# Row scales through DRAM, and squares summed on token-major rows, in a hybrid encoder layer

## The chip, the cores and the metric

The kernel runs on one core of one Trainium2 chip. The metric is the device time of one execution in microseconds (us). The three runs of the kernel before took 768.85, 768.90 and 769.19 us; the median is 768.9.

## The reference, cut to what matters

One layer of an encoder over x (512 tokens, width 1024, float32). What the change touches are two of its norms:

```python
def rmsnorm(x, g):
    xf = x.astype(jnp.float32)
    y = xf * lax.rsqrt(jnp.mean(xf * xf, axis=-1, keepdims=True) + EPS)
    return (y * g.astype(jnp.float32)).astype(x.dtype)

hn = rmsnorm(h, norm_mix_g[l])
proj = hn @ w_in[l]
...
h = h + memory_cross_attention(rmsnorm(h, norm_x_g[l]), mem_n, w_xq[l], w_xkv[l], w_xo[l])
u = rmsnorm(h, norm_ff_g[l]) @ w1[l]
h = h + jnp.square(jax.nn.relu(u)) @ w2[l]
return rmsnorm(h, final_norm_g)
```

Between them stand eight heads of attention with a forget bias, a gated recurrence (HGRN2) over chunks, and attention to 256 memory tokens. The hidden width of the MLP is 4096.

## The kernel before, in words

Activations stand feature-major: 128 features on the partitions, 512 tokens along the free dimension, eight such chunks for the width of 1024. Every matrix product is made of three matmuls per chunk, with each operand split into a high and a low part (`gemm_fm`, lines 236 to 238; 24 matmuls for one product of 128 output features by 512 tokens). Weights come by DMA from SP's queue into two raw buffers, are split by ACT (line 171, names wh) and DVE (line 175, names wl), and the load of the next panel waits for the split of the last but one. PE's order is the order of the code; the other engines are ordered by a scheduler, except in a few blocks written out by hand.

The row scale of a norm is not applied to the activations before the product. The gain is folded into the feature-major activations; the row scale, one number per token, multiplies the product afterwards. Since tokens lie along the free dimension there, the scale must stand in all partitions: a tile `rbc` of 128 x 512, each row the same.

**First norm.** Squares of x are summed on token-major x by ACT and DVE (`x_sq`), which gives `ms0`, 128 x 4, tokens on the partitions. POOL makes the power (`rstd_of`, lines 357 and 360). PE then spreads the 4 columns `r0` to all partitions by four transposes of a broadcast column (line 516, into a PSUM bank of pool `sc`), and DVE copies the bank to `rbc` (line 518). `gate` (line 540) multiplies the first four products `gf` by `rbc`; ACT's sigmoid follows, then `forget`, then the products `gq`. The four `gf` and `gq0` lie in the three banks of the PSUM pool `mm`. Beside this, `x_park` writes the transposed x to DRAM (xTd) from POOL's queue, in four transfers, and POOL loads the bias `fb`.

**MLP's norm.** After cross attention, `residual` adds each chunk of the product with W_xo (names xw) to the residual `hT`, makes the high and low parts `x2_hi` and `x2_lo`, and POOL squares the chunk and adds it to `ssq2` (lines 1073, 1076 and 1077). When three, five and seven chunks are done, `to_tok` transposes two chunks to the token-major accumulator `acc`, whose four tiles (one per 128 tokens) collect the MLP's output; the last two chunks follow after the first product of the MLP. `mean_sq` (line 1087) sums `ssq2` over the partitions on PE by small matmuls, POOL makes the power, and PE and DVE spread the scale as before (lines 1507 and 1508) into the same tile `rbc`. `square` (lines 1305 and 1308) takes max(u, 0) times `rbc` on DVE and squares on ACT, and this frees the product's bank.

**The MLP.** The hidden width is done in eight groups of four products u (group g, half j, column i), with three banks of pool `mm`. For the second matrix, tiles of W2 (names wq) are loaded by SP (`load_raws`), and POOL issues DMAs that add further tiles on top of them (`add_weights`, line 1245), since the product with W2 is made of seven products of sums. `first_adds` issues the first two of a group; `down_raws` is the load followed by them.

Of the kernel before, what the change touches and what calls it, by code (L numbers as in the profile page):

```python
# [42 lines left out]
def emit(  # L43
# [310 lines left out]
    def rstd_of(ms, n, name, r=None):  # L354
# [5 lines left out]
        gp.tensor_tensor(r, e, mhalf[:, 0:n], op=ALU.pow)  # L360
        return r

    def norm_rows(t, name):
        ms = sm(2, name + "m")
        for i in range(2):
            junk = t2(f"{name}j{i}")
            ac.activation(junk, t[:, i * S : (i + 1) * S], AF.Square, scale=1.0 / 32.0, accum_out=ms[:, i : i + 1])
        ve.tensor_tensor(ms[:, 0:1], ms[:, 0:1], ms[:, 1:2], ALU.add)
        r = rstd_of(ms[:, 0:1], 1, name + "r")
        ve.tensor_scalar(t, t, r, None, op0=ALU.mult)  # L370
# [67 lines left out]
    with tc.manual_schedule(engines={mybir.EngineType.Activation, mybir.EngineType.DVE}):  # L438
        ve.tensor_copy(g_mix, gmp)
        x_T(0)  # L440
        warm = mm("warm2")
        for _ in range(WARM2):
            te.matmul(warm, zero[:, 0:P], zero, start=True, stop=True)
        first[0]("v")
        x_hi(0)
        x_lo(0)
        first[0]("l")
        wt0 = stream[0]
        state["used"] = 1
        gfps = [mm(f"gf{i}") for i in range(2)]  # L450

        def first_rows(w, a, start):
            for i in range(2):
                te.matmul(gfps[i], chunk(w, 0, slice(i * P, (i + 1) * P)), a[:, 0, :], start=start, stop=False)

        first_rows(wt0[0], hn_hi, True)
        x_T(1)
        x_hi(1)
        x_lo(1)
        first_rows(wt0[0], hn_lo, False)  # L460
        first_rows(wt0[1], hn_hi, False)
        gfg = [gemm_fm(gfps[i], wt0, i * P, hn_hi, hn_lo, order=range(1, KC), begun=True) for i in range(2)]
        second = []

        def l_soft():

            gps = sc("gps", (33,))
            te.transpose(gps, rows, ident[0:33, 0:33])
            ve.tensor_copy(gv, gps)
            ve.tensor_tensor(lmx, gv[:, 25:29], gv[:, 29:33], ALU.max)  # L470
            ve.tensor_tensor(le, gv[:, 25:33].rearrange("p (r k) -> p r k", r=2), lmx.unsqueeze(1).to_broadcast([P, 2, 4]), ALU.subtract)
            ac.activation(le, le, AF.Exp)
            ve.tensor_tensor(lden, le[:, 0, :], le[:, 1, :], ALU.add)
            ve.reciprocal(lden, lden)
            ve.tensor_tensor(lb, le[:, 0, :], lden, ALU.mult)
            ve.tensor_scalar(oml, lb, -1.0, 1.0, op0=ALU.mult, op1=ALU.add)

        jobs = (
            (first[1],),
            (lambda: x_park(0), lambda: x_park(1), first[2]),  # L480
            (first[3], lambda: second.extend(load_next())),
            (lambda: x_sq(0), lambda: x_park(3)),
            (lambda: x_park(2), lambda: second[0]("h"), lambda: x_sq(2)),
            (lambda: x_sq(1), lambda: second[0]("l"), lambda: x_sq(3)),
            (lambda: second[1]("hl"), l_soft),
            (),
        )
        for c in range(KC):
            for g in gfg if c else ():
                next(g)  # L490
            if c + 2 < KC:
                x_T(c + 2)
                x_hi(c + 2)
                x_lo(c + 2)
            for job in jobs[c]:
                job()
        for g in gfg:
            assert next(g, None) is None
        x_park(7)

        wt1 = stream[1]
        state["used"] = 2
        third = load_next()
        gfps.append(mm("gf2"))
        gf2 = gemm_fm(gfps[2], wt1, 0, hn_hi, hn_lo)
        for _ in range(GF):
            next(gf2)
        r0 = cp.tile([P, NT], F32, name="r0")
        rstd_of(ms0, NT, "r0", r0)

        fb = cp.tile([P, FH], F32, name="fb")
        gp.tensor_copy(fb[:, 0:NT], r0)
        gp.dma_start(fb, fox_f_bias[0].partition_broadcast(P))
        pb = sc("rbc")
        for tb in range(NT):
            te.matmul(pb[:, tb * P : (tb + 1) * P], r0[:, tb : tb + 1].to_broadcast([P, P]), ident, start=True, stop=True)
        rbc = cp.tile([P, S], F32, name="rbc")
        ve.tensor_copy(rbc, pb)
        run_now(gf2)
        gfps.append(mm("gf3"))  # L520
        gf3 = gemm_fm(gfps[3], wt1, P, hn_hi, hn_lo)


        Fg, Mv, Sa, Ag = [], [], [], []
        for hp in range(2):
            Fg.append(s4([2, S], f"F{hp}"))
            Mv.append(s4([2, S], f"mov{hp}"))
            Sa.append(s4([2, S], f"sta{hp}"))

        def kt_(h):  # L530
            return (Sa, Mv)[h % 2][h // 2][:, h % 2, :]

        def qt_(h):
            return (Mv, Sa)[h % 2][h // 2][:, h % 2, :]


        sg = [t2(f"sg{h}") for h in range(4)]

        def gate(h):
            ve.tensor_tensor(sg[h], gfps[h], rbc, ALU.mult)  # L540
            ac.activation(sg[h], sg[h], AF.Sigmoid)

        def forget(h):
            F_ = Fg[h // 2][:, h % 2, :]
            ac.activation(F_, sg[h], AF.Identity, scale=oml[:, h : h + 1], bias=lb[:, h : h + 1])
            ac.activation(kt_(h), F_, AF.Identity, scale=-1.0, bias=1.0)

        x_park(4)
        x_park(6)
        gate(0)  # L550
        gate(1)
        x_park(5)
        third[0]()
        third[1]()
        run_now(gf3)
        gate(2)
        for h in range(3):
            forget(h)
# [3 lines left out]
    for hp in range(2):  # L562
        wt = next_panel()
        for j in range(2):
            h = 2 * hp + j
            ps = mm(f"gq{h}")
            run_now(gemm_fm(ps, wt, j * P, hn_hi, hn_lo))
            ve.tensor_tensor(qt_(h), ps, rbc, ALU.mult)
            ac.activation(qt_(h), qt_(h), AF.Silu)
# [476 lines left out]
    def residual(src_hi, src_lo, g, dst_hi, dst_lo, name, ssq, order, nlast, after=None):  # L1046
# [16 lines left out]
        def rest():  # L1063
            for c in range(KC):
                if c not in gens:
                    open_(c)
                yield from gens[c]
                hc = hTc(c)
                ve.tensor_tensor(hc, hc, ps_[c], ALU.add)  # L1069
                ac.activation(dst_hi[:, c, :], hc, AF.Identity, scale=g[:, c : c + 1])  # L1070
                ve.scalar_tensor_tensor(dst_lo[:, c, :], hc, g[:, c : c + 1], f(dst_hi[:, c, :]), op0=ALU.mult, op1=ALU.subtract)
                if c == 0:
                    gp.tensor_tensor(ssq, hc, hc, op=ALU.mult)
                else:
                    sq = t2(f"{name}sq{c}")
                    gp.tensor_tensor(sq, hc, hc, op=ALU.mult)
                    gp.tensor_tensor(ssq, ssq, sq, op=ALU.add)
                if after is not None and c in (2, 4, 6):
                    after(c - 2)
                    after(c - 1)  # L1080
# [85 lines left out]
    def to_tok(c):  # L1166
# [3 lines left out]
        for tb in range(NT):  # L1170
            d, s_ = acc[tb][:, c * P : (c + 1) * P], ps[:, tb * P : (tb + 1) * P]
            if tb % 2 == 0:
                ac.activation(d, s_, AF.Copy)
            else:
                ve.tensor_copy(d, s_)

    fill.add(x_proj(1), "xq1")
    fill.run(2.0)
    for h in range(4):
        if 0 < h < 3:  # L1180
            fill.add(x_proj(h + 1), f"xq{h + 1}")
        elif h == 3:
            x2_hi, x2_lo = act_tile("x2_hi"), act_tile("x2_lo")
            ssq2 = t2("ssq2")
            early, rest = residual(o_hi, o_lo, g_ff, x2_hi, x2_lo, "xw", ssq2, range(KC), 2, to_tok)
            fill.add(early())
        x_scores(h, 0)
        fill.run(X1)
# [107 lines left out]

    def mlp_up(g, j, wt):
        for i in range(2):
            ps = mm(f"u{g}{j}{i}")
            run_now(gemm_fm(ps, wt, i * P, x2_hi, x2_lo))  # L1300
            yield g, j, i, ps

# [171 lines left out]
    def mlp_up_group(g):  # L1474
        for j in range(2):
            if g < 2:
                wt = next_panel()
                if (g, j) == (0, 0):
                    down_raws(0)
                elif (g, j) == (1, 1):  # L1480
                    for _ in range(2):
                        unit_q.popleft()[1]()
# [14 lines left out]
    rbc2 = rbc  # L1497
    ups = mlp_up_group(0)
    up0 = next(ups)
    ms2 = mean_sq(ssq2, "pm2")  # L1500
    r2 = rstd_of(ms2, NT, "r2")
    to_tok(KC - 2)
    to_tok(KC - 1)
    up1 = next(ups)
    pb = tr("rbc2")
    for tb in range(NT):
        te.matmul(pb[:, tb * P : (tb + 1) * P], r2[:, tb : tb + 1].to_broadcast([P, P]), ident, start=True, stop=True)
    ve.tensor_copy(rbc2, pb)
    square(*up0)
    square(*up1)  # L1510
    for up in ups:
        square(*up)
    hidden_sums(0)
    for name in PRODUCTS:
# [42 lines left out]
```

## Time and profile before

| | us |
|---|---|
| median of three runs | 768.9 |
| the profiled execution's own time | 769.28 |
| its span, first to last instruction | 767.5 |
| busy in it: PE / DVE / ACT / POOL | 759.0 / 523.7 / 368.7 / 190.5 |

The granted clock of TensorE was 0.998 of full speed. In the profile PE is TensorE, DVE VectorE, ACT ScalarE, POOL GpSimd and SP the engine that issues most loads. A row of the timeline has start, duration, engine, line, operation, output and inputs with their shapes, and how many instructions were merged; in brackets stands the idle time ahead of it and what ended it. Matmuls overlap, so the cost of one is the distance between starts. A row of stretches has, after the span, the busy time of PE, of its weight loads, of DVE, ACT and POOL (instructions in parentheses), then the granted clock, the mean busy share of the 16 DMA engines and GB/s. A row of DMA issues ends with the us to landing, the median where there are several.

### The profile page before, as it was taken

What the parts mean: (1) busy time and instruction counts of PE and PEld (TensorE: products, weight loads), DVE (VectorE), ACT (ScalarE), POOL (GpSimd) and SP (SyncE); (2) the same over time, 40 slices, a digit from 0 to 9 for tenths busy, and PEclk for the clock granted to TensorE, in tenths of its full rate; (3) what the DMA queues carried; (4) which work ended last, traced back from release to release, by engine and by line L of the source; (5) the groups of instructions that cost most, each with busy time, mean ns of one, the idle gap of its engine ahead of it and who ended that gap; (6) DMA issues with size and microseconds to landing.
All of it is one profiled execution on the core that took longest, in us unless ns stands there. A gap on an engine that the chain in (4) does not pass through costs nothing.

```text
span 767.5 us, 11244 instructions
## 1 busy us (share of the span) xinstructions
PE 759.0 (99%) x4229; PEld 646.0 (84%) x4229; DVE 523.7 (68%) x849; ACT 368.7 (48%) x620; POOL 190.5 (25%) x264
## 2 busy tenths in 40 slices
PE   9999999999999999999999999999999999999996
PEld 6889888998889988888888888888888888888885
DVE  5747765576787656555548556949596868777696
ACT  5655456665666433344444244435353535342553
POOL 7207432423432025310016510101001010101123
PEclk9999999999999999999999999999999999999999
DMA  8543332232543442231113596565748475757602
GB/s 247 192 136 108 90 84 56 80 114 57 185 149 134 163 139 83 85 100 64 56 56 108 204 262 139 146 158 175 180 149 200 139 174 161 192 137 218 138 1 109
DMA packets 79831, 103.03 MB, mean 134 GB/s; under 512 B 4593, under 2 KB 58394, under 8 KB 79778
## 3 DMA queue, kind: packets, MB, share of 16 engines
q1 hardware_dynamic: 70226, 76.61, 31.1%
q0 software_dynamic: 8960, 24.67, 15.3%
q10 hardware_dynamic: 592, 1.05, 0.4%
q8 instruction: 33, 0.54, 0.3%
q14 instruction: 20, 0.16, 0.1%
HBM read 89.71 MB, written 4.21 MB: 122 GB/s over the span
## 4 chain that ended last, share of the span: by engine, by line
PE 98%; DVE 1%; ACT 1%; POOL 0%; issue 0%; DVEq 0%; ACTq 0%
PE u L238 8%; PE u L236 8%; PE u L237 8%; PE U L1371 4%; PE U L1369 4%; PE U L1370 4%; PE xq L236 2%; PE xq L237 2%; PE xw L236 2%; PE xq L238 2%; PE xw L237 2%; PE xw L238 2%; PE wo L236 2%; PE Y L1371 2%; PE wo L238 2%; PE Y L1370 2%
## 5 line engine op out<-in xcount | busy, mean ns | idle before, releaser
L175 DVE TENSOR_TENSOR wld<-wq,whd 128x1024 fp32r<-128x1024 f32 x56 | 68.6, 1226 | 25.3 <-ACT whd L171 25.2
L236 PE MATMUL u<-x_hi,whu 128*128 128x512 f32 x192 | 74.7, 389 | 0.0
L237 PE MATMUL u<-x_lo,whu 128*128 128x512 f32 x192 | 74.7, 389 | 0.0
L238 PE MATMUL u<-x_hi,wlu 128*128 128x512 f32 x192 | 74.7, 389 | 0.0
L171 ACT ACTIVATE whd<-wq 128x1024 fp32r<-128x1024 f32 x56 | 58.4, 1054 | 30.2 <-PE u L237 18.5
L171 ACT ACTIVATE whu<-wru 128x1024 fp32r<-128x1024 f32 x24 | 25.3, 1053 | 62.1 <-DMA wru<-in_w_dram 62.1
L175 DVE TENSOR_TENSOR wlu<-wru,whu 128x1024 fp32r<-128x1024 f32 x24 | 29.5, 1229 | 32.8 <-ACT whu L171 32.8
L1245 POOL DMA_DIRECT2D wq<-in_w_dram x16 | 19.4, 1242 | 129.1 <-DMA wq<-in_w_dram 117.6
L1369 PE MATMUL U<-whd,hb 128*128 128x512 f32 x120 | 46.7, 389 | 0.0
L1370 PE MATMUL U<-wld,hb 128*128 128x512 f32 x120 | 46.7, 389 | 0.0
L1371 PE MATMUL U<-whd,hb 128*128 128x512 f32 x120 | 46.7, 389 | 0.0
L1245 POOL DMA_DIRECT2D wq<-wq x16 | 14.1, 878 | 123.9 <-DVE wld L175 96.3
L237 PEld LDWEIGHTS u<-x_lo,whu 128*128 128x128 f32 x192 | 36.0, 188 | 7.5
L238 PEld LDWEIGHTS u<-x_hi,wlu 128*128 128x128 f32 x192 | 36.0, 188 | 7.5
L236 PEld LDWEIGHTS u<-x_hi,whu 128*128 128x128 f32 x192 | 36.0, 188 | 7.4
L921 POOL TENSOR_SCALAR bi<-nF,Ft 128x128 f32<-128x128 f32 (+3 forms) x32 | 20.6, 654 | 54.6 <-PE pt L953 34.5
L1308 ACT ACTIVATE sq<-ur 128x512 f32<-128x512 f32 x32 | 20.0, 627 | 26.2 <-DVE ur L1305 26.2
L1305 DVE SCALAR_TENSOR_TENSOR ur<-u,rbc 128x512 f32<-128x512 f32 x32 | 21.9, 688 | 11.5 <-PE u L238 11.5
L1370 PEld LDWEIGHTS U<-wld,hb 128*128 128x128 f32 x120 | 22.5, 188 | 4.7
L1371 PEld LDWEIGHTS U<-whd,hb 128*128 128x128 f32 x120 | 22.5, 188 | 4.7
L1369 PEld LDWEIGHTS U<-whd,hb 128*128 128x128 f32 x120 | 22.5, 188 | 4.6
L1070 ACT ACTIVATE x_hi<-hT,gv 128x512 fp32r<-128x512 f32 x16 | 11.5, 719 | 28.5 <-DVE hT L1069 28.4
(961 smaller groups left out, 2364.2 us busy)
## 6 DMA issues: line engine op xcount, KB each, us to landing
wq<-in_w_dram SPq DMA_DIRECT2D x40, 512.0 KB, 3.3
wru<-in_w_dram SPq DMA_DIRECT2D x24, 512.0 KB, 3.8
wq<-in_w_dram POOLq DMA_DIRECT2D x16, 512.0 KB, 8.2
wq<-wq POOLq DMA_DIRECT2D x16, 512.0 KB, 4.6
xTd<-xT POOLq DMA_DIRECT2D x4, 512.0 KB, 3.3
nF<-Fd POOLq DMA_DIRECT2D x8, 256.0 KB, 3.7
hT<-xTd POOLq DMA_DIRECT2D x4, 512.0 KB, 5.4
xt<-in_x_dram SPq DMA_DIRECT2D x3, 512.0 KB
```

The costliest lines, as they stand in the source:

```text
L171: ac.activation(hi, raw, AF.Copy)
L175: ve.tensor_tensor(lo, raw, f(hi), ALU.subtract)
L236: te.matmul(ps, wh, hi, start=n_ == 0 and not begun, stop=False)
L237: te.matmul(ps, wh, lo, start=False, stop=False)
L238: te.matmul(ps, wl, hi, start=False, stop=k == order[-1])
L921: gp.tensor_scalar(bi[:, 0:n], fF[h][:, 0:n], -1.0, Ft[:, tb, h : h + 1], op0=ALU.mult, op1=ALU.add)
L1245: gp.dma_start(raw.rearrange("p (k n) -> p k n", k=2), src, accum_op=ALU.add)
L1305: ve.scalar_tensor_tensor(u, ps, 0.0, rbc2, op0=ALU.max, op1=ALU.mult)
L1308: ac.activation(sqs[g, j][:, i, :], u, AF.Square)
L1369: te.matmul(ps, hi, whi[:, k, :], start=begin, stop=False, skip_group_check=True)
L1370: te.matmul(ps, hi, wlo[:, k, :], start=False, stop=False, skip_group_check=True)
L1371: te.matmul(ps, lo, whi[:, k, :], start=False, stop=k == 1, skip_group_check=True)
```

## The change

Both scales go to all partitions through DRAM. `on_all` issues two DMAs on POOL's queue: the 128 x 4 scale is written to a row of 512 numbers in DRAM (`Rd`), and that row is read back into all partitions of `rbc`. The transposes on PE and the copies on DVE are gone. The bias `fb` is loaded after the parking of x, the first two gates are written after the split of the third panel, and `gf3` and `gq0` take banks of pool `tr` in place of `mm`.

For the MLP's norm the sums over the partitions on PE and the squares on POOL are gone. Instead `tok_squares` sums the squares of `acc`: when four chunks are there, ACT squares 512 columns of each of the four tiles, and after six and eight chunks DVE adds 256 columns each to the sums. The fourth product of group 0 takes a bank of pool `sc`. The two accumulating loads of group 0 are written after the spreading of the scale, the loads that they add to stay where they were.

```diff
+    Rd = drp.tile([2, S], F32, name="Rd")
+
+    def on_all(i, r, dst):
+
+        gp.dma_start(Rd[i].rearrange("(t p) -> p t", p=P), r)
+        gp.dma_start(dst, Rd[i].partition_broadcast(P))
...
         rstd_of(ms0, NT, "r0", r0)
-
-        fb = cp.tile([P, FH], F32, name="fb")
-        gp.tensor_copy(fb[:, 0:NT], r0)
-        gp.dma_start(fb, fox_f_bias[0].partition_broadcast(P))
-        pb = sc("rbc")
-        for tb in range(NT):
-            te.matmul(pb[:, tb * P : (tb + 1) * P], r0[:, tb : tb + 1].to_broadcast([P, P]), ident, start=True, stop=True)
         rbc = cp.tile([P, S], F32, name="rbc")
-        ve.tensor_copy(rbc, pb)
+        on_all(0, r0, rbc)
         run_now(gf2)
-        gfps.append(mm("gf3"))
+        gfps.append(tr("gf3"))
...
         x_park(4)
         x_park(6)
-        gate(0)
-        gate(1)
         x_park(5)
+
+        fb = cp.tile([P, FH], F32, name="fb")
+        gp.tensor_copy(fb[:, 0:NT], r0)
+        gp.dma_start(fb, fox_f_bias[0].partition_broadcast(P))
         third[0]()
         third[1]()
         run_now(gf3)
+        gate(0)
+        gate(1)
         gate(2)
...
-            ps = mm(f"gq{h}")
+            ps = (mm if h else tr)(f"gq{h}")
...
-                if c == 0:
+                if ssq is None:
+                    pass
+                elif c == 0:
                     gp.tensor_tensor(ssq, hc, hc, op=ALU.mult)
...
+        if c in (3, 5, 7):
+            tok_squares(c)
+
+    ms2 = {}
+
+    def tok_squares(c):
+
+        if c == 3:
+            ms2[c] = sm(NT, "ms2")
+            for tb in range(NT):
+                ac.activation(t2(f"ms2j{tb}"), acc[tb][:, 0:S], AF.Square, scale=1.0 / 32.0, accum_out=ms2[c][:, tb : tb + 1])
+            gp.tensor_scalar(ms2[c], ms2[c], 1.0, EPS, op0=ALU.mult, op1=ALU.add)
+            return
+        cs = slice((c - 1) * P, (c + 1) * P)
+        ms2[c] = sm(NT, f"ms2{c}")
+        for tb in range(NT):
+            a, v = acc[tb][:, cs], (x[:, tb : tb + 1] for x in (ms2[c], ms2[c - 2]))
+            new_, old = v
+            ve.tensor_tensor_reduce(out=t2(f"ms2j{c}{tb}")[:, 0 : 2 * P], in0=a, in1=a, scale=1.0 / D, scalar=old, op0=ALU.mult, op1=ALU.add, accum_out=new_)
...
-            ssq2 = t2("ssq2")
-            early, rest = residual(o_hi, o_lo, g_ff, x2_hi, x2_lo, "xw", ssq2, range(KC), 2, to_tok)
+            early, rest = residual(o_hi, o_lo, g_ff, x2_hi, x2_lo, "xw", None, range(KC), 2, to_tok)
...
-            ps = mm(f"u{g}{j}{i}")
+
+            ps = (sc if (g, j, i) == (0, 1, 1) else mm)(f"u{g}{j}{i}")
...
                 if (g, j) == (0, 0):
-                    down_raws(0)
+                    load_raws(0, RAWS)
...
     up0 = next(ups)
-    ms2 = mean_sq(ssq2, "pm2")
-    r2 = rstd_of(ms2, NT, "r2")
     to_tok(KC - 2)
     to_tok(KC - 1)
-    up1 = next(ups)
-    pb = tr("rbc2")
-    for tb in range(NT):
-        te.matmul(pb[:, tb * P : (tb + 1) * P], r2[:, tb : tb + 1].to_broadcast([P, P]), ident, start=True, stop=True)
-    ve.tensor_copy(rbc2, pb)
-    square(*up0)
-    square(*up1)
-    for up in ups:
+    r2 = sm(NT, "r2")
+    gp.tensor_tensor(r2, ms2[KC - 1], mhalf[:, 0:NT], op=ALU.pow)
+    on_all(1, r2, rbc2)
+    first_adds(0)
+    for up in [up0, *ups]:
         square(*up)
```

How the instructions stand now. First POOL's list around the MLP's norm; before it reads as follows (ssq and xwsq are sums and squares, r2e and r the scale, wq the tiles of W2, where `wq<-in_w_dram` is an accumulating load):

```order
L1076 TENSOR_TENSOR xwsq_4621<-hT_3347 128x512
L1077 TENSOR_TENSOR ssq_4189<-ssq_4189,xwsq_4621 128x512
L357 TENSOR_SCALAR r2e<-pm2m 128x4
L360 TENSOR_TENSOR r_4683<-r2e,mhalf 128x4
L1245 DMA wq_4628<-in_w_dram 128x2x512 x2
L1245 DMA wq_4629<-in_w_dram 128x2x512 x2
L1245 DMA wq_4628<-wq_4628 128x1024
```

And in the changed kernel:

```order
L1242 DMA gfin_4618<-in_final_norm_g_dram 128x512
L1193 TENSOR_SCALAR ms_4484<-ms_4484 128x4
L1269 DMA wq_4621<-in_w_dram 128x2x512 x2
L1528 TENSOR_TENSOR r_4692<-ms_4683,mhalf 128x4
L367 DMA Rd<-r_4692 128x4x1
L368 DMA rbc<-Rd 128x512
L1269 DMA wq_4622<-in_w_dram 128x2x512 x2
```

The squares and sums are gone, the two transfers of the scale are new, and the first pair of accumulating loads stands ahead of the power and of both transfers, though the code has it behind them.

Next DVE's list at the same place, before, from the last low part of the W_xo stage (pm2m is the mean square, acc the copies to token-major, ur the first half of `square`):

```order
L1071 SCALAR_TENSOR_TENSOR x_lo<-hT_3347,gv,x_hi 128x512
L1089 TENSOR_SCALAR pm2m<-pm_4674 128x4
L1175 COPY acc_4354<-ht_4685 128x128
L1175 COPY acc_4354<-ht_4694 128x128
L1175 COPY acc_4356<-ht_4685 128x128
L1175 COPY acc_4356<-ht_4694 128x128
L175 TENSOR_TENSOR wl36a<-wr36a,wh36a 128x1024
L1508 COPY rbc<-rbc_4728 128x512
L175 TENSOR_TENSOR wl36b<-wr36b,wh36b 128x1024
L1305 SCALAR_TENSOR_TENSOR ur_4734<-u_4649,rbc 128x512
```

And in the changed kernel, from the last copy (an ISA row is a sum of squares or the reading of its result):

```order
L1181 COPY acc_4352<-ht_4674 128x128
L1200 ISA ms2j_4686,ms_4683<-acc_4350,ms_4580 128x256
L1200 ISA ms_4683 128x1
L1200 ISA ms2j_4688,ms_4683<-acc_4351,ms_4580 128x256
L1200 ISA ms_4683 128x1
L1200 ISA ms2j_4690,ms_4683<-acc_4352,ms_4580 128x256
L1200 ISA ms_4683 128x1
L175 TENSOR_TENSOR wl36a<-wr36a,wh36a 128x1024
L175 TENSOR_TENSOR wl36b<-wr36b,wh36b 128x1024
L1330 SCALAR_TENSOR_TENSOR ur_4785<-u_4640,rbc 128x512
L1330 SCALAR_TENSOR_TENSOR ur_4789<-u_4698,rbc 128x512
```

The sums of squares stand ahead of both splits of panel 36, and the first `ur` stands behind them without a copy of the scale between.

Last DVE's list at the first norm, before (xT are copies for parking, sg the gates):

```order
L424 COPY xT_363<-xn_327 128x512
L518 COPY rbc<-rbc 128x512
L540 TENSOR_TENSOR sg_419<-gf_220,rbc 128x512
L540 TENSOR_TENSOR sg_420<-gf_221,rbc 128x512
L424 COPY xT_423<-xn_292 128x512
L175 TENSOR_TENSOR wl2a<-wr2a,wh2a 128x1024
L175 TENSOR_TENSOR wl2b<-wr2b,wh2b 128x1024
L540 TENSOR_TENSOR sg_421<-gf_373,rbc 128x512
L540 TENSOR_TENSOR sg_422<-gf_412,rbc 128x512
L175 TENSOR_TENSOR wl3a<-wr3a,wh3a 128x1024
```

And in the changed kernel:

```order
L431 COPY xT_364<-xn_328 128x512
L431 COPY xT_417<-xn_293 128x512
L175 TENSOR_TENSOR wl2a<-wr2a,wh2a 128x1024
L175 TENSOR_TENSOR wl2b<-wr2b,wh2b 128x1024
L540 TENSOR_TENSOR sg_413<-gf_221,rbc 128x512
L540 TENSOR_TENSOR sg_414<-gf_222,rbc 128x512
L540 TENSOR_TENSOR sg_415<-gf_374,rbc 128x512
L540 TENSOR_TENSOR sg_416<-gf_406,rbc 128x512
L175 TENSOR_TENSOR wl3a<-wr3a,wh3a 128x1024
```

All four gates now stand together behind the split of panel 2, and the split of panel 3 behind the four. On POOL the write `Rd<-r` stands directly behind the power, and the read `rbc<-Rd` behind the bias and the third transfer of the parked x; the fourth one stands behind that read.

## The prediction

> **What bounds the kernel now.** The page comes first, then the waits of TensorE (PE).
>
> ```profile
> span 767.5 us, 11244 instructions
> PE 759.0 (99%) x4229; PEld 646.0 (84%) x4229; DVE 523.7 (68%) x849; ACT 368.7 (48%) x620; POOL 190.5 (25%) x264
> PE 98%; DVE 1%; ACT 1%; POOL 0%; issue 0%; DVEq 0%; ACTq 0%
> PE warm L348 <- DVE ones L352: 1.3, 1, 1.3
> PE pst L832 <- DVE rec L853: 0.2, 1, 0.2
> ```
>
> The third row is the chain that ended last, by engine; the last two are all the waits that the trace has for PE, 1.3 us of them before its first instruction. So nearly every microsecond taken from PE's list shortens the run, and every microsecond that PE is made to wait lengthens it. Work moved among DVE, ACT and POOL counts only through such waits. The two places of the change in PE's timeline, the first norm and the MLP's norm:
>
> ```profile
> 24.96 1.12 PE L516 MATMUL rbc<-ident,r 128*128 128x128 f32 x8
> 25.84 0.47 PE L236 MATMUL gf<-hn_hi,wh1b 128*128 128x512 f32 x1
> 26.16 0.39 PE L237 MATMUL gf<-hn_lo,wh1b 128*128 128x512 f32 x1
> 26.38 0.40 PE L238 MATMUL gf<-hn_hi,wl1b 128*128 128x512 f32 x1
> ...
> 436.68 0.95 PE L1087 MATMUL pm<-ones,ssq 128*128 128x1 f32 x8
> 437.48 1.07 PE L1169 MATMUL ht<-ident,hT 128*128 128x128 f32 x8
> ...
> 443.87 1.05 PE L1507 MATMUL rbc<-ident,r 128*128 128x128 f32 x8
> 444.68 0.48 PE L236 MATMUL u<-x_hi,wh35a 128*128 128x512 f32 x1
> 444.99 0.39 PE L237 MATMUL u<-x_lo,wh35a 128*128 128x512 f32 x1
> 445.22 0.39 PE L238 MATMUL u<-x_hi,wl35a 128*128 128x512 f32 x1
> ...
> 455.68 0.39 PE L236 MATMUL u<-x_hi,wh36a 128*128 128x512 f32 x1
> ```
>
> Durations overlap; what a step costs is the distance of starts.
>
> **What goes from PE.** The first broadcast takes 25.84 - 24.96 = 0.88 us, and the matmul behind it comes 0.32 after its forerunner where the next comes 0.22 after: 0.10 more. The sums of squares take 437.48 - 436.68 = 0.80. The second broadcast takes 444.68 - 443.87 = 0.81, and 0.31 against 0.23 behind it is 0.08 more. Together 0.98 + 0.80 + 0.89 = 2.67 us, 0.35% of the run. Nothing is added to PE. This term is firm: the order shows all three steps gone.
>
> **The squares.** The seven squares, seven sums and one first square on POOL go; PE never waited for them (waits above). In their place ACT makes four squares of 512 columns and DVE eight sums of 256.
>
> ```profile
> 18.14 1.22 DVE L433 CUSTOM_DVE_ANT_0 x0j<-xt 128x1024 f32<-128x1024 f32 x1
> 19.29 0.08 DVE L433 DVE_READ_ACCUMULATOR2_ANT ms<- 128x1 f32 x1
> L1308 ACT ACTIVATE sq<-ur 128x512 f32<-128x512 f32 x32 | 20.0, 627 | 26.2 <-DVE ur L1305 26.2
> 396.00:431.00 35.00, 35.00 (x169) 29.23 (x168) 24.91 (x32) 13.56 (x25) 19.43 (x13) 1.00 0.25 76
> ```
>
> ACT's four at 0.63 are 2.5 us (an estimate from the MLP's squares of this shape); the last row is the W_xo stage, where the fourth number after the span is DVE's busy time and the fifth ACT's: 13.56 of 35. DVE's sum over 1024 columns took 1.22 + 0.08; over 256 I take 0.5, between a quarter (0.33) and the whole (1.30). Four of them lie inside this stage, whose DVE has 10 us free: nothing. The last four stand behind the last copies to token-major and are on the way to the scale; they count below. If that cover went, the delay would fall on the split of wh36 behind them, which PE wants only at 455.68.
>
> **The first scale through DRAM.** Before, the first gate follows the copy of the broadcast; now DVE waits at its first gate for two transfers in a row.
>
> ```profile
> 23.79 1.08 POOL L360 TENSOR_TENSOR r<-r0e,mhalf 128x4 f32<-128x4 f32 x1
> fb<-in_fox_f_bias_dram POOLq DMA_DIRECT2D x1, 4.0 KB, 2.9
> Fd<-Fr POOLq DMA_DIRECT2D x1, 16.0 KB, 1.8
> nF<-Fd POOLq DMA_DIRECT2D x2, 256.0 KB, 3.6
> 33.65 0.69 DVE L540 TENSOR_TENSOR sg<-gf,rbc 128x512 f32<-128x512 f32 x1 [0.90 <-PE gf L238]
> 34.37 0.63 ACT L541 ACTIVATE sg<-sg 128x512 f32<-128x512 f32 x1 [0.24 <-DVE sg L540]
> 40.07 1.04 ACT L171 ACTIVATE wh3b<-wr3b 128x1024 fp32r<-128x1024 f32 x1
> 41.15 1.23 DVE L175 TENSOR_TENSOR wl3b<-wr3b,wh3b 128x1024 fp32r<-128x1024 f32 x1 [1.37 <-ACT wh3b L171]
> 47.50 0.39 PE L238 MATMUL gq<-hn_hi,wl3b 128*128 128x512 f32 x1
> ```
>
> The scale is there at 24.87. The write out has no row of its kind; its nearest, the small transfers of POOL's queue, land in 1.8 and 2.9, and I take 2.9. The broadcast back has the shape of nF: 3.6. So rbc lands at 31.4 (30.3 by the shorter row; 34.3 if each of the two takes 2.9 once more behind the residual's parked parts, which share the queue). What is queued behind that wait: the four gates, then on ACT the sigmoids, the forget gates and the splits of wh3. Before, ACT ran from its last sigmoid at 34.37 to the end of wh3b at 41.11, 6.74 us; the three sigmoids and the first forget gate that now stand ahead of that without a pause add 3 x 0.63 + 0.8, so 9.4 us lie between the first product and wh3b. With 0.69 for the product and 1.23 for wl3b, the low halves are ready 11.3 us after rbc: at 42.7. PE wants them at 47.50 - 0.98 = 46.5, so rbc may be as late as 35.2. Cost here: nothing, up to 1 us if my longest case is exceeded. The bank that gate 0 holds is asked for later than that, because gf3 and gq0 now take banks of the pool tr.
>
> **The MLP's scale.** Times are those of before; PE runs 0.98 us earlier from the first broadcast, 1.78 from 436.68, 2.67 from 443.87.
>
> ```profile
> 438.46 1.37 DVE L1175 COPY acc<-ht 128x128 f32<-128x128 f32 x4 [0.64 <-ACT acc L1173]
> 446.70 1.28 DVE L1305 SCALAR_TENSOR_TENSOR ur<-u,rbc 128x512 f32<-128x512 f32 x2
> 438.19 1.03 POOL L360 TENSOR_TENSOR r<-r2e,mhalf 128x4 f32<-128x4 f32 x1
> 439.20 2.54 POOL L1245 DMA_DIRECT2D wq<-in_w_dram  x2
> 431.29 2.60 SPq L1256 DMA_DIRECT2D wq<-in_w_dram  x5
> wq<-in_w_dram SPq DMA_DIRECT2D x5, 512.0 KB, 5.9
> wq<-in_w_dram POOLq DMA_DIRECT2D x2, 512.0 KB, 9.3
> wr37a<-in_w_dram SPq DMA_DIRECT2D x1, 512.0 KB, 7.9
> 438.00:442.00 4.00, 4.00 (x22) 3.38 (x21) 1.07 (x4) 1.86 (x5) 3.66 (x4) 1.00 1.06 380
> 446.00:450.00 4.00, 4.00 (x19) 3.30 (x18) 2.63 (x4) 1.87 (x3) 0.00 (x0) 1.00 1.10 236
> ```
>
> The deadline first. The pool mm has three banks; with the fourth product in sc, the fifth (u of group 1, at 455.68) is the first that needs a bank back, which the square of the first product on DVE frees. PE reaches it at 455.68 - 2.67 = 453.0, so rbc must land by 453.0 - 0.64 (half of the 1.28 for two) = 452.4.
>
> When it lands. The copies end at 439.83 - 1.78 = 438.05; four sums of 0.5 make 440.05. POOL's list now has the two accumulating loads of W2 ahead of the power, as the order shows. They need a2, the third of five loads issued from 431.29: 432.3 + 5.9 = 438.2, and their issue takes 2.54, to 440.7. The power takes 1.03: 441.8. The write of the scale is issued then, behind those two loads on the same queue. They took 9.3 (median of two) to land, in a stretch where the DMA engines are full (last two rows: share 1.06 and 1.10): 438.2 and 439.5 + 9.3 = 447.5 and 448.8. I let the scale's write land with the second, 448.5. The broadcast back, 256 KB, takes 3.6 by nF, where the engines were free, or as long as wr37a of twice the size, 7.9, in this very stretch: 452.1 to 456.4. Midway, 454.2. Then PE waits 454.2 - 452.4 = **1.8 us**; by the ends 0 and 4.0. I take the middle because both rows have a claim: nF by size, wr37a by place. Behind the waiting DVE stand the other squares, the first hidden part and the split wl37; PE wants that split for the third product of group 1, two products of (455.68 - 444.68) / 2 = 5.5 us after the first, so nothing else is late.
>
> The Trainium skill ("DMA: Bandwidth & Descriptors", section on the anatomy of a software-generated DMA) gives each about 2.0 us plus bytes at 436 GB/s; that would make the write 2.0 and the broadcast 2.6, no wait at all and the first rival's time. The trace differs: nF took 3.6, and 512 KB took 7.9 and 9.3 here. The same page's section on queues and rings says that on each DMA engine the descriptors of one ring are consumed in ring order, which speaks for the write standing behind the accumulating loads and so against this change; no row of before has a small transfer behind large ones of its own queue.
>
> **Sum.** -2.67 + 1.8 = -0.9 us. The profiled run took 769.28 with a span of 767.5, 0.4 above the median of 768.9; differences of this size carry over, so 768.9 - 0.9 = **768.0 us**. With the case's ends: 766.2 to 770.2. A measurement of this kernel can tell about 0.2%, 1.5 us, from no change.
>
> **Rivals.** (a) The broadcast is hidden: the scale's write doesn't wait for the accumulating loads, or they drain sooner. Then it lands at 441.8 + 1.8 = 443.6, and rbc at 447.2 to 451.5, ahead of 452.4; only the 2.67 remain: 766.2. For it: the small Fd landed in 1.8. Against it: the full engines and the 9.3. It also takes the lower part of my own interval, waits below 1.1. Chance 0.36.
> (b) My forecast, a wait of 1.1 to 4.2: no change that can be told. Chance 0.42.
> (c) Slower: the write of the scale is the expensive one. It moves 512 single numbers of four bytes. If it and the broadcast each need a loaded landing after the queue has drained, 447.5 + 4.0 (half of 7.9) + 7.9 = 459.4, PE waits 7.0: 768.9 - 2.67 + 7.0 = 773.2. It decides from a landing later than 456.6. The Trainium skill (same page, rules for kernel authors) says that a non-contiguous last dimension lowers to one descriptor per element; no row of before has four-byte pieces. Against it: each piece is tiny and the queue's 4 KB fb landed in 2.9. Chance 0.22.
> That the change doesn't do what it says can't be: the matmuls are gone from PE's order.
>
> **How the numbers follow.** Likeliest 768.0. The range reaches down to (a) in full, 766.0, and up into (c), to 771.0, which leaves about 0.15 out above. Faster 0.36, same 0.42, slower 0.22.
>
> **What would show it.** Right: PE's waits gain one row, u waiting for DVE's ur at about 453, of 1 to 4 us, and the ur before it is put down to the DMA of rbc; the landing of Rd comes after the accumulating loads. Wrong to the good: no such row, Rd landed in about 2. Wrong to the bad: a wait of 5 or more there, or a PE wait at gq between 38 and 47, which would say that the first scale has no cover either.

## The result, and the profile after

The changed kernel takes 787.22 us (median of five runs, 787.08 to 787.97) beside 769.14 for the kernel before on the same chip: a ratio of 1.0236, 95% interval 1.0224 to 1.0247. It is slower by 18.1 us; the forecast was 768.0, with a range up to 771.0. The profiled execution has a span of 785.5 where before had 767.5.

The page's first lines and the chain that ended last:

```profile
span 785.5 us, 11195 instructions
PE 761.0 (97%) x4205; PEld 645.9 (82%) x4205; DVE 517.4 (66%) x862; ACT 370.4 (47%) x628; POOL 170.5 (22%) x253
PE 88%; DMA 4%; issue 3%; ACT 2%; DVE 2%; POOL 1%; SPq 0%; ACTq 0%; DVEq 0%; POOLq 0%
```

The two longest waits of PE:

```profile
PE u L236 <- DVE ur L1330: 10.6, 1, 10.6
PE gq L236 <- DVE sg L540: 5.6, 1, 5.6
```

PE has 24 matmuls fewer and yet is busy 2.0 longer, and the chain that ended last, 98% PE before, now has 88% PE and 4% DMA. Both waits are new, one at each norm. The first norm in the timeline (POOL, DVE, then PE):

```profile
23.56 1.08 POOL L360 TENSOR_TENSOR r<-r0e,mhalf 128x4 f32<-128x4 f32 x1
24.94 0.84 POOL L367 DMA_DIRECT2D Rd<-r  x1 [0.30 <-POOL r L360]
36.30 0.54 POOL L368 DMA_DIRECT2D rbc<-Rd  x1 [8.91 <-DMA Rd<-r]
...
42.68 2.48 DVE L540 TENSOR_TENSOR sg<-gf,rbc 128x512 f32<-128x512 f32 x4 [13.09 <-DMA rbc<-Rd]
...
52.58 1.23 DVE L175 TENSOR_TENSOR wl3b<-wr3b,wh3b 128x1024 fp32r<-128x1024 f32 x1 [2.09 <-ACT wh3b L171]
...
37.41 0.39 PE L238 MATMUL gq<-hn_hi,wl2b 128*128 128x512 f32 x1
43.43 0.80 PE L236 MATMUL gq<-hn_hi,wh2a 128*128 128x512 f32 x1 [5.63 <-DVE sg L540]
44.02 0.63 PE L237 MATMUL gq<-hn_lo,wh2a 128*128 128x512 f32 x1
44.45 0.63 PE L238 MATMUL gq<-hn_hi,wl2a 128*128 128x512 f32 x1
...
49.12 0.40 PE L237 MATMUL gq<-hn_lo,wh2b 128*128 128x512 f32 x1
49.35 0.40 PE L238 MATMUL gq<-hn_hi,wl2b 128*128 128x512 f32 x1
```

The write of the scale is issued at 24.94, as forecast, but the broadcast that reads it back can only be issued at 36.30. DVE's gates wait until 42.68, and PE stands from 37.6 to 43.43, 5.8 us, for the bank that the first gate frees 0.75 after `rbc` lands. The matmuls after that are 0.63 long and 0.43 apart where they were 0.39 and 0.23. The MLP's norm (POOL, DVE, PE):

```profile
445.70 2.55 POOL L1269 DMA_DIRECT2D wq<-in_w_dram  x2 [19.70 <-DVE acc L1181]
448.08 1.23 POOL L1528 TENSOR_TENSOR r<-ms,mhalf 128x4 f32<-128x4 f32 x1
449.62 0.83 POOL L367 DMA_DIRECT2D Rd<-r  x1 [0.30 <-POOL r L1528]
465.21 0.58 POOL L368 DMA_DIRECT2D rbc<-Rd  x1 [14.77 <-DMA Rd<-r]
...
446.09 0.48 DVE L1200 CUSTOM_DVE_ANT_0 ms2j<-acc,ms 128x256 f32<-128x256 f32 x1
471.46 1.29 DVE L1330 SCALAR_TENSOR_TENSOR ur<-u,rbc 128x512 f32<-128x512 f32 x2 [18.26 <-DMA rbc<-Rd]
...
461.28 0.39 PE L238 MATMUL u<-x_hi,wl35b 128*128 128x512 f32 x1
472.30 0.77 PE L236 MATMUL u<-x_hi,wh36a 128*128 128x512 f32 x1 [10.62 <-DVE ur L1330]
472.86 0.63 PE L237 MATMUL u<-x_lo,wh36a 128*128 128x512 f32 x1
...
475.81 0.40 PE L238 MATMUL u<-x_hi,wl36a 128*128 128x512 f32 x1
```

Again the write is late, and PE stands 10.8 us. The landings, from the DMA view of the stretches 24 to 40 and 436 to 470 (last number, us from issue):

```profile
Rd<-r POOLq DMA_DIRECT2D x1, 2.0 KB, 11.1
rbc<-Rd POOLq DMA_DIRECT2D x1, 256.0 KB, 6.4
fb<-in_fox_f_bias_dram POOLq DMA_DIRECT2D x1, 4.0 KB, 10.3
...
Rd<-r POOLq DMA_DIRECT2D x1, 2.0 KB, 15.3
rbc<-Rd POOLq DMA_DIRECT2D x1, 256.0 KB, 6.2
wr37a<-in_w_dram SPq DMA_DIRECT2D x1, 512.0 KB, 14.8
```

Two kilobytes took 11.1 and 15.3, 1.7 and 2.5 times what the 256 KB behind them took. The first broadcast took 6.4 where 3.6 was forecast. Other transfers were late beside them: fb took 10.3 (2.9 before), and wr37a of SP's queue 14.8 (7.9 before).

The sum: PE's gaps are, with 0.23 for the usual distance between starts, 43.43 - 37.41 - 0.23 = 5.79 and 472.30 - 461.28 - 0.23 = 10.79. The slow matmuls, 13 distances in the first place and 8 in the second, cost (49.12 - 43.43) - 13 x 0.227 = 2.74 and (475.81 - 472.30) - 8 x 0.227 = 1.69. With the 2.67 that went from PE: 5.79 + 10.79 + 2.74 + 1.69 - 2.67 = 18.3, beside 18.0 of the spans.

### The profile page after: what moved, and what is told of

The parts are those of the page before. It is cut to its first block, busy times and chain, and to the rows that moved or that the text cites. A ratio compares the mean times of both kernels' runs of the same rounds, so it can differ in the third digit from the quotient of the medians.

```text
span 785.5 us, 11195 instructions
## 1 busy us (share of the span) xinstructions
PE 761.0 (97%) x4205; PEld 645.9 (82%) x4205; DVE 517.4 (66%) x862; ACT 370.4 (47%) x628; POOL 170.5 (22%) x253
## 4 chain that ended last, share of the span: by engine, by line
PE 88%; DMA 4%; issue 3%; ACT 2%; DVE 2%; POOL 1%; SPq 0%; ACTq 0%; DVEq 0%; POOLq 0%
PE u L236 7%; PE u L238 7%; PE u L237 7%; PE U L1396 3%; PE U L1395 3%; PE U L1394 3%; PE xq L236 2%; PE xq L237 2%; PE xw L236 2%; PE xq L238 2%; PE xw L238 2%; PE xw L237 2%; PE wo L236 2%; PE Y L1396 2%; PE wo L238 2%
## 5 line engine op out<-in xcount | busy, mean ns | idle before, releaser
L1330 DVE SCALAR_TENSOR_TENSOR ur<-u,rbc 128x512 f32<-128x512 f32 x32 | 21.9, 687 | 25.7 <-DMA rbc<-Rd 18.3
L1394 PE MATMUL Y<-whd,hb 128*128 128x512 f32 x64 | 24.9, 389 | 0.0
```

The source lines that it names most:

```text
L1330: ve.scalar_tensor_tensor(u, ps, 0.0, rbc2, op0=ALU.max, op1=ALU.mult)
L1394: te.matmul(ps, hi, whi[:, k, :], start=begin, stop=False, skip_group_check=True)
```

## Experiments

**Which part loses.** Each half of the change alone: in the first kernel the MLP's norm is that of before, in the second the first norm.

```
e2_first_only: before.py + on_all(0, r0, rbc), the moved gates and fb, tr banks
e3_mlp_only:   after.py, first norm, gates, fb and banks as in before.py
```

> Only the first norm's scale goes through DRAM; the MLP's norm is as in the kernel before. If the two places lose independently: PE waits about 5.6 at gq, the clock after it costs about 2.6, 0.98 goes from PE, so about +7.2 and 776.3 us. Rival: the whole loss is the MLP's and the first stage recovers later: within 1 us of the kernel before.

> Only the MLP's norm is changed; the first norm is as in the kernel before. If the two places lose independently: PE waits about 10.6 at u, the clock after it costs about 1.6, 1.69 goes from PE, so about +10.5 and 779.6 us. Rival: the write landed late in the changed kernel because the first stage's delay shifted loads against it; then the wait is well below 10 and the time below 776.

Measured: 775.78 us (ratio 1.0089, 1.0072 to 1.0106) and 777.67 us (1.0117, 1.0098 to 1.0135), beside 769.21 for the kernel before, timed with them.

```profile
PE gq L236 <- DVE sg L540: 4.0, 1, 4.0
```

```profile
PE u L236 <- DVE ur L1333: 8.4, 1, 8.4
```

Both halves lose, 6.6 and 8.5, so the rival of the first falls. The second lies between its forecast, 779.6, and its rival, below 776; but its write took 14.5 without the first norm's delay, so that delay is not what makes it late. Together the halves lose 15.0 of 18.1: the waits are 4.0 and 8.4 where the whole change has 5.6 and 10.6, since the writes landed in 10.1 and 14.5 in place of 11.1 and 15.3, and the broadcasts in 5.7 and 4.6 in place of 6.4 and 6.2. Why they landed sooner is not shown.

**What is slow in the write.** Writes that nobody waits for were added to the kernel before, in the attention to memory.

```diff
+        d = drp.tile([S], F32, name=f"pd{n}")
+        v = sm(NT, f"pv{n}")
...
+        for i in range(2):
+            gp.tensor_copy(v[:, 2 * i : 2 * i + 2], den)
...
+            nt = {2: 1, 3: 2}.get(n, NT)
+            gp.dma_start(d.rearrange("(t p) -> p t", p=P)[:, 0:nt], v[:, 0:nt])
```

> The kernel before with seven unused writes to DRAM added in the attention to memory (about 320 to 400 us), where the DMA engines are busy a fifth of the time; nobody waits for them, so the time should be the kernel before's within 1 us. Theory A (the pieces of four bytes are what is slow): 512 pieces of four bytes land about 11 us after issue here too, 256 pieces about 6, 128 pieces about 3 to 4, 128 pieces of 16 bytes also 3 to 4, four rows of 512 bytes about 2. Theory B (the write was slow because it stood behind other transfers of its queue): all of them land in 2 to 3, since nothing stands ahead. Theory C (any round trip through DRAM is slow): all of them take 8 or more. One of the writes of 512 pieces is issued by ACT in place of POOL: if the software queue is the cause, that one alone lands in 2 to 3.

Measured: the time stayed (768.92, one run, beside 769.21; the other kernels with such writes have one run each too). The landings of 512 pieces from POOL, of 512 from ACT's queue, and of four rows of 512 bytes:

```profile
pd<-pv POOLq DMA_DIRECT2D x1, 2.0 KB, 11.3
pd<-pv ACTq DMA_DIRECT2D x1, 2.0 KB, 8.6
pd<-xp POOLq DMA_DIRECT2D x1, 2.0 KB, 1.7
```

So theory B as the whole cause falls (nothing stood ahead) and theory C falls (the four rows took 1.7); the software queue is not the cause either. But theory A's price for each piece falls too: 128 pieces took 8.3, 256 took 10.8, 512 took 11.3, 10.1 and 9.5. (The 256, and the 512 with 10.1, were issued while another such write was still on its way.) The 128 pieces of 16 bytes were issued 3 us behind the 512 and landed with them, so they told nothing of their own. What the late write does to others is seen from SP's load of wr30a, issued at 340.9 in both kernels. Stretches of before, then of the kernel with the writes, whose first one is on its way until 333.7 + 11.3 = 345.0 (last two numbers: DMA share and GB/s):

```profile
341.00:343.00 2.00, 2.00 (x11) 1.65 (x10) 1.03 (x1) 1.96 (x3) 0.00 (x0) 1.00 0.46 134
343.00:345.00 2.00, 2.00 (x16) 1.88 (x15) 1.94 (x4) 0.66 (x2) 0.00 (x0) 1.00 0.72 245
```

```profile
341.00:343.00 2.00, 2.00 (x11) 1.65 (x10) 1.07 (x1) 1.96 (x3) 0.00 (x0) 1.00 0.04 8
343.00:345.00 2.00, 2.00 (x16) 1.88 (x15) 1.94 (x4) 0.61 (x2) 0.00 (x0) 1.00 0.10 2
345.00:347.00 2.00, 2.00 (x11) 1.66 (x10) 0.95 (x3) 0.81 (x3) 0.00 (x0) 1.00 0.87 258
```

The load of another queue stands nearly still, with the DMA engines idle by their records, until the write has landed. The Trainium skill ("DMA: Bandwidth & Descriptors", section "Back-pressure in remote DMA") says that stalled writes stall the other queues of the same DMA engine; it says so of writes between cores, and here a load stood still beside a core's own write to DRAM; that a stall of the write held it is not shown.

Four further kernels made such writes one at a time, to find what shape is slow. The shape is that of the DRAM tile and of the slice; the first line below is 128 pieces at a distance of w x 4 bytes, the second n pieces side by side, the third n rows of w numbers.

```diff
+        gp.dma_start(drp.tile([P, w], F32, name=f"pd{h}")[:, 0:1], v[:, 0:1])
+        gp.dma_start(d.rearrange("(p t) -> p t", t=1), v[0:n, 0:1])
+        gp.dma_start(drp.tile([n, w], F32, name=f"pd{h}"), pr_[0:n, 0, 0:w])
```

> Again unused small writes in the attention to memory, now one at a time, about 15 us apart. The first probes showed that 128 pieces of four bytes take 8.3 and 512 take 9.5 to 11.3, so the number of pieces is not the main cost. Theory A1 (a write to DRAM in pieces that are too short waits some 8 us for its completion, however many they are): 128 pieces of 16 bytes land in 8 to 11, 128 pieces of four bytes that each have 512 bytes of DRAM to themselves in about 8, 16 pieces of four bytes in about 8, 128 pieces of four bytes from SBUF to SBUF in about 2. Theory A2 (128 source partitions are what is slow): 8, 8, 2 to 3, 8. Theory A3 (many pieces fall into the same line of DRAM and wait for each other): 8, about 2, 2 to 8, 2.

> Four more unused writes to DRAM, one at a time: 32 rows of 64 bytes, 8 rows of 256 bytes, 128 rows of 64 bytes, 128 rows of 512 bytes. Theory A1 (pieces too short): about 8 for those of 64 bytes, 8 or 2 for those of 256, which tells how short is too short, and 2 to 3 for 128 rows of 512. Theory A2 (128 source partitions): about 2, 2, 8, 8. Theory A3 (the same line): about 2 for all that fill whole lines, if a line has 64 bytes.

> Unused writes of 128 pieces of four bytes, one at a time in the quiet stage, at a distance of 64, 32, 16 and 8 bytes in DRAM. So far 512 bytes apart took 3.1 and side by side 8.3, while 16 pieces side by side took 1.6 and 128 pieces of 16 bytes 2.2. Theory A3 (pieces that share a line of 64 bytes are written one after the other, about 0.5 us each): 1.7 to 3 at 64, then about 0.5 more for each further piece in a line: 2.5, 3.5, 5.5. If only the lack of a gap counts (the DMA engines run into each other on neighbouring pieces): all four in 3 or less.

> Unused writes of 32, 64, 128 and 512 pieces of four bytes side by side, one at a time. Theory A3 by pieces in a line (16 in each here): 8 or more for all four, though 16 pieces in one line took 1.6. If the cost comes with the number of DMA engines that write into one line, it rises with the number of pieces from 1.6 for 16 to 8 for 128, and stays at 9 to 11 for 512.

Measured, in us to landing. The second of the four places in each kernel is marked *, since the times are longer there: one and the same write of 128 x 16 bytes, made at each place of the last kernel of this kind, took 2.2, 3.4*, 1.7 and 1.8. While this write is on its way there, and at none of the other places, the trace has a packet of an instruction queue; that this is the cause is not shown.

| rows or pieces that are no shorter than 16 bytes | us |
|---|---|
| 128 x 512 B; 128 x 64 B; 32 x 64 B; 8 x 256 B | 1.8; 1.8; 1.7; 3.2* |
| 128 x 16 B | 2.2 |

| pieces of four bytes | us |
|---|---|
| 128, a piece every 512, 64, 32, 16 bytes | 3.1*, 1.8, 3.2*, 1.7 |
| 128, a piece every 8 bytes | 4.9 |
| side by side: 16, 32, 64, 128, 512 pieces | 1.6, 3.4, 6.4*, 7.5, 8.8 |
| 128, from SBUF to SBUF | 1.7 |

Theory A1 falls (128 short pieces 16 bytes apart took 1.7) and so does A2 (128 partitions, 1.8). A3 comes nearest, since it is the density that counts, but not in its form: two and four pieces in 64 bytes cost nothing, and 16 pieces in one line took 1.6. That a gap between the pieces is enough, the other expectation there, falls too: 4.9 at a distance of 8 bytes. The rise with the number of pieces came as expected, but whether the number of DMA engines in a line makes it is not shown. What is slow is many four-byte numbers at 8 bytes or less in DRAM. That is the layout of Rd.

The last kernel of this kind asked whether the order of the pieces matters; sd is a copy of the column in DRAM.

```diff
+        if h in (0, 3):
+            gp.dma_start(d.rearrange("(p t) -> p t", t=1), sd[:, 0:1])
+        else:
+            gp.dma_start(d.rearrange("(a b t) -> b a t", b=16, t=1), sd[:, 0:1].rearrange("(a b) t -> b a t", b=16))
```

> Unused writes of 128 pieces of four bytes that fill 512 bytes of DRAM, copied from DRAM so that the order is free: the first and the last in the order of the addresses, the two between them in steps of 64 bytes (eight pieces, then the next eight). If a wait between neighbouring pieces that follow each other is the cause: 7 to 9 for the first and the last, 2 to 4 for the two between. If the memory is slow on short pieces that lie densely, in any order: 7 to 9 for all four.

Measured: 7.5 and 8.8 in the order of the addresses, 6.7* and 7.3 in steps of 64 bytes (the write with 8.8 stood behind two loads of 256 KB on its queue). The order does not make it slow: dense short pieces are slow whichever comes first. What in the memory makes them so stays open.

**The write as four rows.** PE turns the 128 x 4 scale, and Rd is written in rows of 512 bytes; nothing else in the path changes, except that the MLP's second product stands ahead of the turn.

```diff
+        ps = (sc, tr)[i](f"rT{i}")
+        te.transpose(ps[0:NT, 0:P], r, ident)
+        rT = t2(f"rTs{i}")[0:NT, 0:P]
+        ve.tensor_copy(rT, ps[0:NT, 0:P])
-        gp.dma_start(Rd[i].rearrange("(t p) -> p t", p=P), r)
+        gp.dma_start(Rd[i].rearrange("(t p) -> t p", p=P), rT)
```

> The changed kernel, but PE transposes the 128 x 4 scale first, DVE copies it, and the write to DRAM has four rows of 512 bytes in place of 512 pieces of four bytes; for the MLP the transpose stands behind the second product. Theory A: the writes land in about 2, PE waits nothing at gq and 0 to 3 at u, and the time is 767 to 770 us. Theory B: fast at the first norm, 10 to 15 for the MLP's write behind the accumulating loads, a wait of 5 or more at u, 773 to 778. Theory C: both land in 11 to 15 as in the changed kernel, 785 or more.

Measured: 772.20 us (ratio 1.0043, 1.0028 to 1.0058, beside 769.21), between the times of A and B. The landings at the first and the MLP's norm, and PE's one wait:

```profile
Rd<-rTs POOLq DMA_DIRECT2D x1, 2.0 KB, 2.1
...
Rd<-rTs POOLq DMA_DIRECT2D x1, 2.0 KB, 7.2
```

```profile
PE u L236 <- DVE ur L1334: 3.0, 1, 3.0
```

At the first norm A holds: 2.1 in place of 11.1, and no wait at gq. At the MLP the write still takes 7.2, more than A says and less than B. The loads that add, ahead of it on POOL's queue, may be a second cause there. Two kernels move them behind both transfers, one with rows and one with pieces.

```diff
-    on_all(1, r2, rbc2)
-    first_adds(0)
+    with tc.manual_schedule(engines={mybir.EngineType.Pool}):
+        on_all(1, r2, rbc2)
+        first_adds(0)
```

> The kernel with rows of 512 bytes, in which the MLP's write still took 7.2 behind the two accumulating loads and PE waited 3.0; now these loads stand behind both transfers of the scale on POOL. If the queue's order held the write: it lands in about 2 here as at the first norm, the broadcast in 4 to 6, PE's wait at u goes, the clock stays, and the time is 766.5 to 767.8 us. If the full DMA engines held it, whatever the queue's order: it lands in 5 or more again, PE waits 2 or more, and the time stays at 771 to 772.

> The changed kernel, pieces of four bytes kept, with the two accumulating loads behind both transfers of the scale on POOL. If pieces and queue add up at the MLP's write (14.5 with both, 7.2 with rows behind the loads, 4.5 with rows ahead of them): the write lands in about 10 to 12, the wait at u falls from 10.6 to 4 to 7, and the time to 780 to 784 us. If the queue alone held it there: about 4.5, no wait at u, 775 to 776.

Measured with rows: 767.08 us beside 769.43, ratio 0.9969 (0.9958 to 0.9980): the one version here that carries the whole change and beats the kernel before by more than a measurement leaves open. No wait at gq or u is left. With pieces: 781.07 in one run. Landings of the MLP's write and broadcast with rows, then the write and PE's wait with pieces:

```profile
Rd<-rTs POOLq DMA_DIRECT2D x1, 2.0 KB, 4.5
rbc<-Rd POOLq DMA_DIRECT2D x1, 256.0 KB, 3.6
```

```profile
Rd<-r POOLq DMA_DIRECT2D x1, 2.0 KB, 9.2
```

```profile
PE u L236 <- DVE ur L1330: 4.8, 1, 4.8
```

So the MLP's write takes 4.5 (rows, loads behind), 7.2 (rows, loads ahead), 9.2 (pieces, loads behind), 14.5 to 15.3 (both). So the loads ahead are a second cause, 2.7 with rows and 5.3 to 6.1 with pieces. Rows ahead of the loads still took 4.5 and not 2, in a stretch where the DMA engines are full (share 0.95 and 1.03 from 440 to 448); that comes near the rival's 5, but PE does not wait for it. The pieces took 9.2 where 10 to 12 were expected.

**The clock.** Unused matmuls fill the two stalls of the changed kernel.

```diff
+            if h == 1:
+                keep(hn_hi, 24)
...
+            if (g, j, i) == (1, 0, 0):
+                keep(x2_hi, 46)
```

> The changed kernel with unused matmuls where PE stalls: 24 ahead of the second gq (5.5 us), 46 ahead of the fifth u (10.5 us). If the granted clock falls because PE stands idle: it stays above 0.95 in both places, the 4.2 us that the slow matmuls cost go, and the time is 782.5 to 784. If the clock falls for another reason (the burst on DVE and ACT behind the scale, the DMA): it falls to 0.5 as before, and the time is 786.5 to 789.

Measured: 783.87 us beside 787.22 for the changed kernel, which was timed on another chip with the kernel before at 769.14 there and 769.43 here. The granted clock (third number from the end) stayed at 1.00, where the changed kernel had 0.50 and 0.53. First the kernel with the unused matmuls, then the changed kernel:

```profile
44.00:48.00 4.00, 4.00 (x20) 3.30 (x19) 0.91 (x1) 4.00 (x7) 0.00 (x0) 1.00 0.02 4
472.00:476.00 4.00, 4.00 (x20) 3.30 (x18) 2.35 (x4) 2.95 (x4) 0.00 (x0) 1.00 0.15 28
```

```profile
44.00:48.00 4.00, 4.00 (x11) 3.15 (x10) 1.17 (x2) 4.00 (x8) 0.00 (x0) 0.50 0.00 0
472.00:476.00 4.00, 3.70 (x9) 3.00 (x10) 2.04 (x4) 2.42 (x5) 0.00 (x0) 0.53 1.06 194
```

The clock falls because PE stands, and a stall costs more than its length: 3.4 us less here against the 4.4 of the sum above. PE has a new wait here, 0.5 for the split `wl3b`; the rest of the difference is not shown. The Trainium skill ("TensorE: Matmul & The Clock Gate", section "Part 1: The HAM clock gate") says that the clock halves after an idle window of about 3.4 us and comes back after about as long a busy one; the rows agree on the half, and the slow stretch lasted 5.7 and 3.5 us. A gap of 3.1 us, shorter than that window, was enough in the kernel with rows (last section).

**The sums alone.** The kernel before with the squares summed on token-major rows, both scales spread by PE; the bank of pool `sc` and the later place of the accumulating loads are those of the change.

```diff
-    ms2 = mean_sq(ssq2, "pm2")
-    r2 = rstd_of(ms2, NT, "r2")
+    r2 = sm(NT, "r2")
+    gp.tensor_tensor(r2, ms2[KC - 1], mhalf[:, 0:NT], op=ALU.pow)
```

> The kernel before with one part of the change alone: squares summed on token-major rows, so that the 0.80 of the small matmuls goes from PE; both scales are spread by PE as before. By the working on record: -0.80, 768.6 us beside 769.4 for the kernel before, just at what a measurement can tell. Rival: the sums on ACT and DVE cost a wait somewhere: 769.4 or more.

Measured: 768.47 beside 769.24, ratio 0.9989 (0.9980 to 0.9998): -0.77, as the rows said.

## Why the prediction was wrong

The step that failed is the landing of the write: "The write out has no row of its kind; its nearest, the small transfers of POOL's queue, land in 1.8 and 2.9, and I take 2.9", and for the MLP "I let the scale's write land with the second, 448.5". It took 11.1 and 15.3. Those two rows are small and of the same queue, as the write is, but they do not have its shape in DRAM: fb is read from DRAM, and Fd is written in eight rows of 2 KB. With no row of dense short pieces, the upper bound of 2.9 was no bound; it should have stayed open. For a write in rows the queueing step was right: behind the loads it took 7.2, beside 448.5 - 441.8 = 6.7 forecast.

| step | forecast | measured |
|---|---|---|
| removed from PE | -2.67 | the sums alone -0.77 for 0.80; the whole change with rows and late loads -2.35, two transposes added |
| squares on DVE, each | 0.5 | 0.48 + 0.08, no wait |
| first write landed, after | 2.9 | 11.1 |
| first broadcast | 3.6 | 6.4 |
| first scale in all partitions at | 31.4, 35.2 at the latest | 42.7 |
| first norm | nothing | 5.8 of stall, 2.7 of clock |
| MLP's power done, behind the loads | 441.8 | 449.3, with 8.5 of it from the first norm |
| MLP's write landed | 448.5 | 464.9, 7.9 too late after the same 8.5 |
| MLP's broadcast | 3.6 to 7.9 | 6.2 |
| PE waits at u | 1.8 | 10.8, and 1.7 of clock |

The deadlines were right, but at the first norm the one that stopped PE was not the one that the prediction priced. The 35.2 is that of the low halves, and its chain came out (11.3 from `rbc` to the end of `wl3b` forecast, 53.81 - 42.68 = 11.1 measured); the bank of gate 0, "asked for later than that", was asked for at 37.64, so `rbc` had to land by 37.64 - 0.75 = 36.9, and 42.7 - 36.9 is the stall of 5.8. The low halves cost nothing on top, since PE came 8.5 later to them; so that a scale 7.5 late for 35.2 cost 8.5 is chance. The claim "Cost here: nothing" fell with the write: with 2.9 for it, even a broadcast of 6.4 lands at about 34.5, an estimate from the issue at 24.94. The MLP's scale was 8.7 later than forecast beyond the 8.5, and the wait grew from 1.8 to 10.8. Both signs of "wrong to the bad" came, the wait above 5 at u and the wait at gq. Two slips of the working stand aside from this: two transfers that are each 2.9 later make 37.2, not 34.3, so that this longest case was already beyond 35.2; and the second load's 448.8 went on as 448.5.

The queueing behind the loads was a true term, but the smaller one: rows ahead of them or behind differ by 2.7, pieces by 5 to 6, while pieces and rows differ by 4.7 ahead of the loads and by 7.3 to 8.1 behind them. Wrong by omission was the clock: no step gave a stall a price beyond its length.

Rival (c) named the right transfer, "512 single numbers of four bytes". It stands beside the rule of the Trainium skill ("DMA: Bandwidth & Descriptors", section "Rules for kernel authors") that such a transfer becomes one descriptor per element; but single elements alone do not make it slow, since 128 of them 16 bytes apart took 1.7. The rival then priced the write by a loaded landing of 4.0, at one norm only. Its 773.2 plus 3.8 (wait 10.8, not 7.0), 1.7 (clock) and 8.5 (first norm) is 787.2. The argument against it, that fb's 4 KB landed in 2.9, was the same wrong row. Rival (a), that the write does not wait for the loads, comes near only with rows and with the loads moved: 767.08 beside its 766.2.

## What to carry to other kernels

Take the price of a small transfer from a row with the same piece size and spacing at its DRAM end, not from one of the same size and queue; where no such row exists, leave the bound open upward and look first at who waits. Turn a column of numbers into rows before it goes to DRAM: here that made 2.1 of 11.1 us, and with the large loads issued behind it the change became a gain of 0.3%. Price a stall of PE with the slow matmuls behind it, 1.7 to 2.7 us here.

## What the runs showed of the hardware

- Many four-byte numbers side by side in DRAM land late, 7.5 to 11.3 us for 128 to 512 of them, whichever queue issues them (128 in steps of 64 bytes: 6.7 and 7.3); 16 bytes apart 128 of them took 1.7, and rows of 64 bytes 1.7 to 1.8.
- While such a write was on its way, a load of another queue moved at 2 to 8 GB/s in place of 134 to 245, though the DMA engines were recorded as nearly idle: the busy share does not show the hold.
- A gap of PE of 3.1 us was enough for the half clock, which came 0.9 us after PE had started again. From the kernel with rows, whose loads stand ahead:

```profile
453.15 0.39 PE L238 MATMUL u<-x_hi,wl35b 128*128 128x512 f32 x1
456.52 0.47 PE L236 MATMUL u<-x_hi,wh36a 128*128 128x512 f32 x1 [2.98 <-DVE ur L1334]
457.06 0.54 PE L238 MATMUL u<-x_hi,wl36a 128*128 128x512 f32 x1
457.39 0.63 PE L236 MATMUL u<-x_hi,wh36a 128*128 128x512 f32 x1
...
460.70 0.40 PE L238 MATMUL u<-x_hi,wl36a 128*128 128x512 f32 x1
```
